# A hybrid attention and state-space layer: the context's norm and the state space's parameters made among the first norms

## The chip, the core and the metric

The kernel runs on one core of a Trainium2 chip. The metric is device time in microseconds for one execution. A core has five engines with instruction queues of their own: TensorE (PE, its weight loads are shown as PEld), VectorE (DVE), ScalarE (ACT), GpSimd (POOL) and SyncE (SP), which issues most of the transfers here. Everything is fp32; where a product must be exact enough, each factor is split into a high and a low part and three matmuls are made of one.

## What is computed

One layer of a diffusion backbone over 1024 tokens and 256 context tokens of 1024 channels. The part of the reference that matters:

```python
mod_x = silu(c) @ w_mod + b_mod;  mod_c = silu(c_ctx) @ w_mod + b_mod
px = modulate(rmsnorm(x, g_norm_mix), sh1, sc1) @ w_in
pc = modulate(rmsnorm(ctx, g_norm_mix), ch1, cc1) @ w_in
y_conv = conformer_conv(conv_x, ...);  y_fnet = fourier_mix(fnet_x, ...)
y_na   = neighbourhood_attention(q, k, v, kc, vc, rpb)
y_ssm  = s5_bidirectional(ssm_x, ssm_c, a_re, a_im, log_dt, b, c, d, ...)
out = group_rmsnorm(concat(y_conv, y_fnet, y_na, y_ssm)) @ w_out + b_out
x = x + gt1 * out;  x = x + gt2 * mlp(modulate(rmsnorm(x), sh2, sc2))
```

The state space (S5) has 16 groups of 16 channels with 64 complex states in two directions. Its context scan runs first and gives the token scan its first state. From a_re, a_im and log_dt come, once for the layer, the step's decay and angle, their powers up to 9, and the discretised B: here called the parameters.

## The kernel before, in words

`body` traces the whole program. A planner then sets the order of the instructions on each engine: it keeps to the data's dependencies and the tiles' buffers, prefers what was traced earlier, and lets later work in where an engine would stand idle by its own estimates. Waits between engines are put in by the framework. Only from the attention on is TensorE's order written out by hand, and in the MLP that of four engines. So a step that stands earlier in the source has precedence there, and does not have to run there. Each engine's queue is in order once it is made; `tc.issue_after(ins)` makes what its block traces on the engine of `ins` stand behind `ins`.

The stages, by what they compute:

- First norms (from L297). x is loaded in two halves of 512 tokens, its squares are summed (ACT and DVE, L206 to L210). For each of eight channel chunks k the shift and scale are made on TensorE from `wmodA` (`gemv`, L149 and L155; loads L299; `set_mod` L160, `gsc` L316), and the chunk is normalised in `normchunk`: `nt` on DVE (L215), `xh` on ACT (L218), `xl` on DVE (L220). The weights of tiles 12, 13 (state space) and 8 (keys) are loaded in this loop and split by ACT (L233) and POOL (L235).
- Tokens' projections: `x_tile` makes 24 matmuls (L364) for a tile of 128 output channels and one half. First come tiles 12, 13 and 8 for both halves; `ev_ssm` writes the state-space channels to `us_d` in DRAM, `ev_k` the keys to `k_d`.
- Context: `ctt` (L401) is loaded into a pool opened after the first norms' pool is closed; then four modulation blocks, the context's norm (`modnorm`), and its projections `c_tile` (L242 to L244) for tiles 12 and 13 (stored to `us_d` by L423) and 8 (`k_ctx`), then five modulation blocks. A modulation block (`mods`, L340 to L357) loads 512 KB of `wmodB` into a buffer that the weights share (three buffers), makes a gemv on TensorE (L344), copies the row on ACT and turns it with two small matmuls (L349).
- Parameters (L436 to L581): some ninety small operations on POOL (`E_ = G`) and DVE, 16 columns wide, hopping between the two; two sines on ACT; powers `pw` by `cmul`, copied to `pa` and `pb` by DVE (L552 to L556); `bb` and `bm` on POOL.
- State space, eight batches of two groups: `ssm_setup` (L607 to L651: tables of weights on POOL and DVE, kernel matmul `pk` L635, transposes `pt`, copies on ACT, and a trip of the kernel through DRAM), `ssm_tables` (phases and sines, L656 to L672), `ssm_main` (`U` from `us_d` L679, state matmul `ps` L686, a rotation and scan on DVE and POOL L692 to L709, output matmul `py` L713 to L717, store to `ys_d`).
- Filling in beside it and behind it: one modulation block, tile 9 (keys), tiles 4 and 5 (Fourier) with two blocks behind each half, the values (L760), the first convolution input `conv_in(0)` (its gate is L787), the state space's output gate (GLU), the Fourier mixing, `conv_in(1)`, the queries (tiles 6 and 7) with a modulation block behind each half, and the convolution's taps of the first half of the channels (L1012 to L1023, one DVE instruction of 512 columns a tap).
- Attention with the output projection beside it (its first DVE step is L1249), then the MLP.

`mods` makes 16 blocks at most in this phase; the other 16 are made in the attention.

## Time and profile before

| what | value |
|---|---|
| median of 3 runs | 1310.3 us (1308.32 to 1315.78) |
| the profiled execution | 1304.56 us, span 1302.6 us |
| TensorE busy in the span | 1184.6 us (91%) |
| DVE, POOL, ACT busy | 1003.8, 767.1, 645.0 us |
| mean granted TensorE clock | 0.954 of full speed (2.4 GHz) |

The profile is of one execution. Times in it count from the start of the span. A line number L is that of the kernel's file; a helper that makes many instructions gives them all one line, so names of tiles matter as much. "Busy" says nothing of why an engine is idle; the views of waits name the instruction whose end was waited for. The granted clock is the share of full speed that TensorE was allowed; it has two levels, 1.2 and 2.4 GHz, and a mean between them says how long it was at which.

### The profile page before, as it was taken

Reading aid. Unit: us, or ns where it says so; the run is one execution under the profiler, and the core shown is the slowest. Engines: PE = TensorE matmul, PEld = TensorE weight load, DVE = VectorE, ACT = ScalarE, POOL = GpSimd, SP = SyncE. Lnnn points to the kernel's source line nnn. Section 1 sums busy time; section 2 is a strip of 40 time slices with the busy share of each in tenths; the row PEclk is TensorE's granted clock in tenths of the full one; section 3 lists DMA queues with packets and bytes.
Section 4 is the critical chain, followed back from the end, with each engine's and each line's share of the span. In section 5 each row is a group of like instructions: output and inputs, shape, how many; then the busy total and the mean of one; then the engine's idle time right before and its main releaser. Section 6 shows DMA issues by size and latency. Waiting matters only on the chain.

```text
span 1302.6 us, 18800 instructions
## 1 busy us (share of the span) xinstructions
PE 1184.6 (91%) x6252; PEld 962.1 (74%) x6252; DVE 1003.8 (77%) x1604; ACT 645.0 (50%) x1335; POOL 767.1 (59%) x1004
## 2 busy tenths in 40 slices
PE   4988988998866898998999999999999999999995
PEld 2776677876646787877777788888887888877875
DVE  5557789689988868758696487787787787787767
ACT  5343343323345655644664355555445555445564
POOL 2138787472556733015268377777777777777654
PEclk9888989998975999998999999999999999999998
DMA  9455342261154644324021111112211111211113
GB/s 362 139 193 157 101 121 70 68 204 55 41 165 136 172 134 119 114 81 146 25 74 41 57 51 38 52 56 65 65 53 37 50 57 65 65 40 42 57 41 130
DMA packets 75058, 121.75 MB, mean 93 GB/s; under 512 B 16977, under 2 KB 35154, under 8 KB 74962
## 3 DMA queue, kind: packets, MB, share of 16 engines
q1 hardware_dynamic: 62802, 113.22, 27.9%
q10 hardware_dynamic: 12160, 7.34, 1.8%
q8 instruction: 49, 0.80, 0.3%
q14 instruction: 47, 0.39, 0.1%
HBM read 106.66 MB, written 13.88 MB: 93 GB/s over the span
## 4 chain that ended last, share of the span: by engine, by line
PE 57%; DVE 21%; ACT 6%; DMA 4%; issue 3%; POOL 3%; SPq 0%; ACTq 0%; DVEq 0%; POOLq 0%
PE fa L1477 12%; PE qa L1477 6%; PE fb L1477 6%; PE qb L1477 6%; DVE cacc L1020 3%; PE qc L1477 3%; PE fc L1477 3%; PE p_t L1275 2%; PE mm L1102 2%; PE mm L1477 2%; PE f L1477 1%; DMA kr<-k_d 1%; PE p_t L1263 1%; DVE fl L1493 1%; PE mm L364 1%
## 5 line engine op out<-in xcount | busy, mean ns | idle before, releaser
L1461 POOL TENSOR_TENSOR w2l<-w2r,w2h 128x128 fp32r<-128x128 f32 (+1 forms) x232 | 174.1, 752 | 78.0 <-ACT w2h L1460 71.8
L1498 DVE SCALAR_TENSOR_TENSOR X<-fa,gt2c,X 128x512 f32<-128x512 f32 x216 | 159.5, 745 | 14.4 <-PE fa L1477 14.4
L1460 ACT ACTIVATE w2h<-w2r 128x128 fp32r<-128x128 f32 (+1 forms) x232 | 85.9, 387 | 134.3 <-POOL w2r L1714 69.7
L235 POOL TENSOR_TENSOR wlo<-wraw,whi 128x1024 fp32r<-128x1024 f32 x30 | 73.6, 2456 | 120.0 <-ACT whi L233 96.5
L1461 POOL TENSOR_TENSOR w2l<-w1r,w2h 128x256 fp32r<-128x256 f32 x136 | 102.2, 766 | 65.2 <-ACT w2h L1460 41.3
L1498 DVE SCALAR_TENSOR_TENSOR X<-fb,gt2c,X 128x512 f32<-128x512 f32 x108 | 80.6, 746 | 41.5 <-PE fb L1477 40.7
L1461 POOL TENSOR_TENSOR w2l<-ws,w2h 128x256 fp32r<-128x256 f32 x84 | 68.0, 816 | 39.1 <-ACT w2h L1460 20.4
L1020 DVE SCALAR_TENSOR_TENSOR cacc<-cv,wdw,cacc 128x512 f32<-128x512 f32 x92 | 87.2, 994 | 0.4
L364 PE MATMUL mm<-xh,whi 128*128 128x512 f32 x192 | 79.0, 428 | 6.4 <-ACT xh L218 4.8
L364 PE MATMUL mm<-xl,whi 128*128 128x512 f32 x192 | 80.5, 419 | 0.5 <-DVE xl L220 0.5
L364 PE MATMUL mm<-xh,wlo 128*128 128x512 f32 x192 | 79.6, 416 | 0.0
L1460 ACT ACTIVATE w2h<-w1r 128x256 fp32r<-128x256 f32 x136 | 54.0, 410 | 51.0 <-DVE w1r L1614 19.7
L1477 PE MATMUL qa<-cb,w2h 128*128 128x512 f32 x224 | 70.6, 396 | 0.7 <-ACT ft L1629 0.7
L1477 PE MATMUL fa<-th,w2h 128*128 128x512 f32 x156 | 62.1, 398 | 0.0
L1477 PE MATMUL fa<-th,w2l 128*128 128x512 f32 x156 | 61.4, 393 | 0.7 <-POOL w2l L1461 0.7
L1477 PE MATMUL fa<-tl,w2h 128*128 128x512 f32 x156 | 61.5, 394 | 0.0
L1018 POOL TENSOR_TENSOR pacc<-pacc,ptmp 128x512 f32<-128x512 f32 x24 | 39.6, 1649 | 27.7 <-ACT ptmp L1017 27.7
L1460 ACT ACTIVATE w2h<-ws 128x256 fp32r<-128x256 f32 x84 | 33.1, 410 | 42.7 <-DVE ws L1610 19.6
L364 PEld LDWEIGHTS mm<-xh,whi 128*128 128x128 f32 x192 | 38.2, 201 | 17.5 <-ACT xh L218 5.3
L1477 PEld LDWEIGHTS qa<-cb,w2h 128*128 128x128 f32 x224 | 42.0, 188 | 11.3 <-ACT ft L1629 1.1
L233 ACT ACTIVATE whi<-wraw 128x1024 fp32r<-128x1024 f32 x30 | 31.7, 1056 | 31.9 <-DMA wraw<-in_w_out 10.6
L1498 DVE SCALAR_TENSOR_TENSOR X<-fc,gt2c,X 128x512 f32<-128x512 f32 x56 | 41.9, 749 | 6.9 <-PE fc L1477 2.4
(799 smaller groups left out, 3847.0 us busy)
## 6 DMA issues: line engine op xcount, KB each, us to landing
w2r<-in_w_ff SPq DMA_DIRECT2D x68, 256.0 KB
wmB<-in_wmodB SPq DMA_DIRECT2D x32, 512.0 KB
w1r<-in_w_ff SPq DMA_DIRECT2D x64, 256.0 KB
wm<-in_wmodA SPq DMA_DIRECT2D x16, 512.0 KB
wraw<-in_w_in SPq DMA_DIRECT2D x12, 512.0 KB
x<-in_xT SPq DMA_DIRECT2D x8, 512.0 KB
wraw<-in_w_out SPq DMA_DIRECT2D x8, 512.0 KB
kr<-k_d SPq DMA_DIRECT2D x16, 256.0 KB
```

Source lines behind the costliest of these rows:

```text
L233: S.activation(hi, raw, AF.Copy)
L235: (lo_eng or G).tensor_tensor(lo, raw, hi.bitcast(F32), ALU.subtract)
L364: PE.matmul(o, a_[:, k, :], b_[hf][k], start=k == 0 and i == 0, stop=k == 7 and i == 2)
L1018: G.tensor_tensor(pacc, pacc, t, ALU.add)
L1020: V.scalar_tensor_tensor(acc, x(k), w(k), acc, ALU.mult, ALU.add)
L1102: PE.matmul(o, a_[:, 2 * kk + c, :], b_, start=c == 0 and i == 0, stop=c == 1 and i == 2)
L1263: PE.transpose(pT[:, i * P:(i + 1) * P], pr_[:, i * P:(i + 1) * P], ident)
L1275: PE.matmul(po[:, j * 64:j * 64 + 64], ptt[:, i * P:(i + 1) * P], rv, start=i == 0, stop=i == 4, skip_group_check=True)
L1460: S.activation(hi, a, AF.Copy)
L1461: G.tensor_tensor(lo, a, hi.bitcast(F32), ALU.subtract)
L1477: PE.matmul(o, a_[:, i, :], m_, start=start and j == 0, stop=stop and j == 2, skip_group_check=True)
L1498: return V.scalar_tensor_tensor(x, o, gt2(k), x, ALU.mult, ALU.add).ins
```

## The change

- A pool `xc` for the context is opened ahead of the first norms' pool. `ctt` is loaded into it in front of the modulation weights of chunk 3 (k == 3), the context's squares and reciprocal root are made at k == 5, and its eight chunks are normalised right behind the loop. `ctt`, `ch` and `cl` keep their shapes.
- The state space's parameters become a function, traced behind the norm of chunk 1. Their five loads (`log_dt` twice, B twice, C) stand behind the identity's and ahead of the first modulation weights. The arithmetic is the same; the eight copies into `pa` and `pb` go from DVE to POOL. `ssm_setup` becomes a function traced earlier (it is called where it was), and its tiles `ca`, `cx`, `kt_`, `tz`, `wt` move to the pool opened after the parameters' small pool is closed.
- Behind the first norms the order is: tiles 12 and 13 for both halves, the context's tiles 12 and 13, tile 8 for both halves, the context's tile 8. The nine modulation blocks that stood there are taken out.
- Of the 16 modulation blocks nine are now traced with tiles 9, 4 and 5, one behind `conv_in(0)`, one ahead of `conv_in(1)`, four with the queries, the rest ahead of the taps. SP's part of the block with tiles 9, 4 and 5 (their loads but for tile 9's weights, which stand ahead) is queued behind the first load of `U`.

The diff, without the lines that only move:

```diff
+    cts = ExitStack()
+    xc = open_pool("ctxc", "left", stack=cts)
...
+    def ssm_loads():
+        ldt = tn("ldt")
+        for d in range(2):
+            SP.dma_start(ldt[d * 64:(d + 1) * 64, :], ap(A["log_dt"], d * 16, [[0, 64], [1, 16]]))
...
+        for i in range(2):
+            SP.dma_start(bn[i], A["bnat"][:, i, :])
+        SP.dma_start(cn, A["cnat"])
...
+    def ssm_params():
...
         for dst, src in ((pa_r, pw_r), (pa_i, pw_i)):
-            V.tensor_copy(dst[0:64], src[0:64])
-            V.tensor_copy(dst[64:128], src[64:128, ::-1, :])
+            G.tensor_copy(dst[0:64], src[0:64])
+            G.tensor_copy(dst[64:128], src[64:128, ::-1, :])
...
     load_x(0)
     SP.dma_start(ident, A["cst"][:, 0:P])
+    ssm_loads()
+    ctt = []
     for k in range(8):
+        if k == 3:
+            for i in range(8):
+                ctt.append(xc.tile([P, TC], F32, name="ctt", tag="hc", bufs=16))
+                SP.dma_start(ctt[i], A["ctxT"][:, i, :])
         wm = load_wm(k)
...
         norm_x(0, pbs[0], k)
+        if k == 1:
+            ssm_params()
...
+        if k == 5:
+            pbc = rstd_bc(xc, sumsq(xc, ctt, TC), TC, 0, st_tile, NM)
+            pbs.append(xc.tile([P, TC], F32, name="pbc"))
+            S.copy(pbs[2], pbc[:, :TC])
+    ch, cl = zip(*[normchunk(xc, ctt[k], TC, gsc[:, k, 1:2], mod[:, 0, k, 1:2], pbs[2], "c", "hc", xc) for k in range(8)])
     st.close()
...
-    for hf in range(2):
-        for ti in FIRST:
-            o = x_tile(cw[ti], hf, (("mm", "gn"), ("at", "gv"))[hf][ti == 8])
...
-    mods(4)
-    ch, cl = modnorm(xp, sumsq(xp, ctt, TC), ctt, TC, ...
+    for hf in range(2):
+        for ti in FIRST[:2]:
+            ev_ssm(ti - 12, hf, x_tile(cw[ti], hf, first_tag(ti, hf)))
     for m in range(2):
         o = c_tile(cw[12 + m])
...
+    for hf in range(2):
+        ev_k(8, hf, x_tile(cw[8], hf, first_tag(8, hf)))
+    gvp = ps_tile("gv", "gvp")
...
     k_ctx(8)
-    mods(5)
...
-            SP.dma_start(U[:, g, 0:160], ap(us_d, ...
+            ld = SP.dma_start(U[:, g, 0:160], ap(us_d, ...
+        state_in.append(ld.ins)
...
-    mods(1)
     cw[9] = load_w(A["w_in"][9])
-    for hf in range(2):
-        ev_k(9, hf, x_tile(cw[9], hf))
-    k_ctx(9)
-    mods(0)
-    for ti in (4, 5):
-        w = load_w(A["w_in"][ti])
+    with tc.issue_after(state_in[0]):
+        mods(1)
         for hf in range(2):
-            ev_u(ti, hf, x_tile(w, hf))
-            mods(2)
+            ev_k(9, hf, x_tile(cw[9], hf))
+        k_ctx(9)
+        for ti in (4, 5):
+            w = load_w(A["w_in"][ti])
+            for hf in range(2):
+                ev_u(ti, hf, x_tile(w, hf))
+                mods(2)
...
     conv_in(0)
+    mods(1)
...
+    mods(1)
     conv_in(1)
...
-    mods(1)
+    mods(2)
     for _ in tap_steps(0, 0):
```

## Rows read from the trace of the kernel before

**Rows 1.** The page's first part: busy time, share of the span, instructions
```profile
PE 1184.6 (91%) x6252; PEld 962.1 (74%) x6252; DVE 1003.8 (77%) x1604; ACT 645.0 (50%) x1335; POOL 767.1 (59%) x1004
```

**Rows 2.** Windows by stage: PE, PEld, DVE, ACT, POOL busy; granted clock; DMA share, GB/s
```profile
37.00:78.00 41.00, 40.74 (x226) 30.72 (x225) 21.07 (x45) 12.66 (x24) 2.57 (x7) 0.94 0.42 132
78.00:130.00 52.00, 42.95 (x360) 34.07 (x362) 36.39 (x94) 22.50 (x55) 37.93 (x90) 0.80 0.59 187
130.00:205.00 75.00, 64.54 (x475) 49.75 (x472) 62.49 (x90) 30.63 (x68) 60.82 (x67) 0.95 0.36 108
205.00:264.50 59.50, 59.20 (x405) 50.59 (x404) 42.64 (x76) 20.12 (x42) 32.12 (x37) 0.97 0.25 72
264.50:391.00 126.50, 99.84 (x444) 80.81 (x443) 120.12 (x148) 46.17 (x70) 65.23 (x38) 0.89 0.36 115
```

**Rows 3.** Timeline of DVE: start, us, engine, line, operation, out<-in, count, [idle before it <-releaser]
```profile
264.59 0.69 DVE L787 SCALAR_TENSOR_TENSOR cv<-cth,mm 128x512 f32<-128x512 f32 x1 [5.75 <-PE mm L364]
...
391.10 0.82 DVE L1249 CUSTOM_DVE_ANT_0 pr__3575<-p_s,bt 128x640 f32<-128x640 f32 x1
```

**Rows 4.** Chain of waits, 98 to 131 us: start, duration, what
```profile
99.52 4.52 DMA us_d<-pC
...
104.47 3.15 DMA us_d<-pC
```

**Rows 5.** Timeline of SP, POOL and DVE: the parameters
```profile
69.32 1.20 SPq L446 DMA_DIRECT2D t_ldt<-in_log_dt  x2
...
73.56 0.20 POOL L451 TENSOR_SCALAR t_dn<-t_ldt 128x16 f32<-128x16 f32 x1 [34.68 <-DMA t_ldt<-in_log_dt]
...
102.75 0.71 DVE L553 COPY pa_i<-pw_i 64x160 f32<-64x160 f32 x1
```

**Rows 6.** Views by tile: state matmul, output matmul; first and last start
```profile
L686 PE MATMUL ps<-U,wt x128: 297/298/350, 129.7 to 243.8; 128*64 128x159 f32 x128
...
L717 PE MATMUL py<-hr,cx x64: 273/275/421, 143.5 to 258.4; 128*128 128x128 f32 x64
```

**Rows 7.** Windows, the parameters' new and old place
```profile
18.00:37.00 19.00, 12.87 (x75) 7.61 (x76) 14.13 (x23) 9.72 (x17) 4.38 (x2) 0.86 0.90 347
73.50:106.00 32.50, 26.79 (x259) 21.50 (x257) 20.40 (x72) 14.96 (x38) 20.86 (x72) 0.84 0.59 184
```

**Rows 8.** Waits of PE, 70 to 265 us: in total, times, longest
```profile
PE pg L344 <- DMA wmB<-in_wmodB: 3.5, 1, 3.5
...
PE ps L686 <- ACT wt L651: 2.5, 1, 2.5
...
PE pg L344 <- ACT gv_rows L357: 1.4, 1, 1.4
```

**Rows 9.** Timeline of PE behind a gap; chain of waits at 248
```profile
116.02 0.63 PE L364 MATMUL mm<-xh,whi 128*128 128x512 f32 x1
...
116.86 0.40 PE L364 MATMUL mm<-xh,wlo 128*128 128x512 f32 x1
...
247.99 8.64 PE mm L364 x37
```

**Rows 10.** Timeline of PE: one modulation block
```profile
99.26 0.39 PE L349 MATMUL gvp<-cst,gv_rows 128*128 128x2 f32 x2
99.58 0.64 PE L344 MATMUL gvp<-wmB,sT 128*32 128x128 f32 x16
```

**Rows 11.** Timeline of SP, 15 to 60 us
```profile
15.56 1.67 SPq L570 DMA_DIRECT2D bn<-in_bnat  x2
...
27.12 23.68 SPq L299 DMA_DIRECT2D wm<-in_wmodA  x8
```

**Rows 12.** Timeline: a DVE instruction beside a POOL split and alone
```profile
110.04 2.19 DVE L660 TENSOR_SCALAR p<-ph 128x318 f32<-128x318 f32 x1 [0.20 <-ACT ph L659]
...
120.18 0.32 DVE L660 TENSOR_SCALAR p<-ph 128x318 f32<-128x318 f32 x1
...
109.61 2.43 POOL L235 TENSOR_TENSOR wlo<-wraw,whi 128x1024 fp32r<-128x1024 f32 x1
```

More of the change, by code (lines that the diff above doesn't have):

```diff
@@ L306, in add_rstd, with tn @@
         S.copy(pbs[hf], rstd_bc(p1, pbs[hf], H, 0, (mm_tile, at_tile)[hf], NS))
+    sset = ExitStack()
+    sp = open_pool("ssm", "right", stack=sset)
+    tst = ExitStack()
+    tp = open_pool("tiny", "right", stack=tst)
+    GB = 2
+    NB_ = 16 // GB
+    fl = lambda t: t.rearrange("p g q -> p (g q)")
+    v4 = lambda t: t.rearrange("p g (s m) -> p g s m", m=16)
+    b3 = lambda t: t.rearrange("p (g m) -> p g m", g=16)
+    PR = {}
+    def tn(name, pool=None):
+        return (pool or tp).tile([P, 16], F32, name="t_" + name)
@@ new lines, in ssm_loads @@
+    def ssm_loads():
+        ldt = tn("ldt")
+        for d in range(2):
+            SP.dma_start(ldt[d * 64:(d + 1) * 64, :], ap(A["log_dt"], d * 16, [[0, 64], [1, 16]]))
+        bn = [sp.tile([P, 2, 160], F32, name="bn", tag="ss", bufs=4).rearrange("p a b -> p (a b)")[:, :256]
+              for _ in range(2)]
+        cn = sp.tile([P, 2, 256], F32, name="cn")
+        for i in range(2):
+            SP.dma_start(bn[i], A["bnat"][:, i, :])
+        SP.dma_start(cn, A["cnat"])
+        PR["loads"] = ldt, bn, cn
@@ L397, in body @@
     SP.dma_start(colf, A["cols"][:, NCOLS - 40:])
-    ctt = []
-    for k in range(8):
-        ctt.append(xp.tile([P, TC], F32, name="ctt", tag="hc", bufs=16))
-        SP.dma_start(ctt[k], A["ctxT"][:, k, :])
-    for hf in range(2):
-        for ti in FIRST:
-            o = x_tile(cw[ti], hf, (("mm", "gn"), ("at", "gv"))[hf][ti == 8])
-            if ti >= 12:
-                ev_ssm(ti - 12, hf, o)
-            else:
-                ev_k(ti, hf, o)
-    gvp = ps_tile("gv", "gvp")
-    mods(4)
-    ch, cl = modnorm(xp, sumsq(xp, ctt, TC), ctt, TC,
-                     lambda k: gsc[:, k, 1:2], lambda k: mod[:, 0, k, 1:2], "c", "hc", xp, pt=st_tile)
     def c_tile(w):
@@ L561, in body @@
-    tt(rho, rho, rho, ALU.mult)
-    E_.tensor_scalar(th8, tau, 8.0, 1.0, ALU.mult, ALU.mult)
-    frac(th8)
-    E_.tensor_scalar(th_h, th8, 1536.0, 1536.0, ALU.add, ALU.subtract)
-    tt(th_l, th8, th_h, ALU.subtract)
-    bn = [sp.tile([P, 2, 160], F32, name="bn", tag="ss", bufs=4).rearrange("p a b -> p (a b)")[:, :256]
-          for _ in range(2)]
-    cn = sp.tile([P, 2, 256], F32, name="cn")
-    for i in range(2):
-        SP.dma_start(bn[i], A["bnat"][:, i, :])
-    SP.dma_start(cn, A["cnat"])
@@ L572, in body @@
-    b3 = lambda t: t.rearrange("p (g m) -> p g m", g=16)
-    bc16 = lambda t: t[:, :, None].to_broadcast([P, 16, 16])
-    bb_r = sp.tile([P, 16, 16], F32, name="bb_r")
-    bb_i = sp.tile([P, 16, 16], F32, name="bb_i")
-    cmul(bb_r, bb_i, bc16(zr), bc16(zi), b3(bn[0]), b3(bn[1]), None, "ss", G)
-    tst.close()
-    bm = sp.tile([P, 2, 16, 32], F32, name="bm")
-    G.memset(bm[:, :, :, 16:32], 0.0)
-    G.tensor_copy(bm[:, 0, :, 0:16], bb_r)
-    G.tensor_copy(bm[:, 1, :, 0:16], bb_i)
-    GB = 2
@@ L721, in ssm_main @@
             S.dma_start(ap(ys_d, (GB * b + g) * 16 * 1024, [[128, 8], [1024, 16], [1, 128]]), yt[:, g, :])
+    rho, th_h, th_l = PR["rho"], PR["th_h"], PR["th_l"]
+    for _ in range(3):
+        new_cx(sp2)
     ready = [ssm_setup(0) + ssm_tables(0)]
```

347 lines of the change are left out of this document (178 added, 169 removed).

## The prediction

> **What bounds the kernel now.** I read the page first, then the stages, then the waits of the second and third stage. By the page TensorE is busy for 91% of the span [rows 1]. That is an average, and the change touches only what lies before the attention, so I cut the span into stages [rows 2]. The reader is to see three kinds. From 37 to 78 us TensorE is full (40.74 of 41.00 us) and POOL nearly empty (2.57). From 78 to 130 TensorE has holes (42.95 of 52.00), its granted clock falls to 0.80, and POOL is busy with small things. From 264.5 to 391 DVE is full (120.12 of 126.50) and TensorE isn't. After 391 come attention and MLP, which the change leaves alone. So the question is when DVE's last stage can begin: it begins with the convolution's gate at 264.59 us, after an idle 5.75 us that ended with the TensorE tile of that gate [rows 3]. Whatever brings that tile forward brings the end forward.
>
> What holds it back is in the chain of waits [rows 4]: at 99.52 and 104.47 us it stands on the two stores of the context's projected channels into us_d (4.52 and 3.15 us), then on DVE's and ACT's setup work. The parameters are late because log_dt is asked for at 69.32 us only; POOL sits idle for 34.68 us before its first use, and the last power copy is done at 102.75 + 0.71 = 103.46 [rows 5]. The first state matmul (ps) starts at 129.7, the last output matmul (py) at 258.4 [rows 6].
>
> **Parameters and context norm, moved.** In the old place, from 73.5 to 106, POOL is busy 20.86 us and DVE 20.40 us, DVE's with the context's norm [rows 7]; eight power copies go from DVE to POOL, about 0.5 us each by the last one's 0.71. In the new place they stand beside 37 to 78, where DVE is idle for 41.00 - 21.07 = 19.9 us and POOL for 38 [rows 2]: they fit, at no cost of their own. What the move frees on TensorE is the gaps of 78 to 130, which sum to 52.00 - 42.95 = 9.05 us. The waits say why [rows 8]: the longest are modulation matmuls waiting for their weights (3.5) or for a copy (1.4), because nothing else is ready while the context's tiles wait for their norm. In the new order the projections of the tokens (tiles 8 and 9) stand there. I take 8 us; between 4 (half the waits come back) and 9.
>
> **Clock.** Granted 0.80 over those 52 us means 1.2 GHz for 2 x 0.20 = 40% of them; 40% of 42.95 busy us is 17.2, of which half, 8.6, is what the low clock cost. The level was low behind a 3.5 us wait [rows 8] and came back when TensorE had been busy again (the same matmul takes 0.63 us, then 0.40) [rows 9]. With the gaps gone I take 7; between 3 and 8.6.
>
> **Modulations.** Before, the 16 modulation blocks of this phase are issued ahead of the first convolution input. After it, nine are issued among tiles 9, 4 and 5 and seven behind the first convolution input, in the stage where TensorE has 126.50 - 99.84 = 26.7 idle us. A block is 0.64 us of gemv and 0.39 us of selection [rows 10], overlapping slightly: 7 x 0.95 = 6.6 us leave the path to 264.5 (5 to 7). Their seven weight loads and copies move with them and fall under DVE's taps; if that cover fails, because they share a PSUM bank with the group norms, it costs the 6.6 again.
>
> **The state space's lead.** Setup of batch 0 no longer waits for the context, so wt is there before U. The 2.5 us that ps once waited for wt [rows 8], and about 1.5 us of low clock behind that gap, go: 4 us. The bounds are 0 and everything that 130 to 264.5 still holds: 10.5 + 0.3 idle, and 3.8 + 1.8 from clocks 0.95 and 0.97 [rows 2], 16 us in all. I take the small value because the other waits there are of the batches on themselves (hr, Ss, yt).
>
> **The added wait.** The modulations' loads and the weights of tiles 4 and 5 are queued on SP behind batch 0's U load, which waits for the pC stores. TensorE waits for them. The cover is tiles 8 and 9 with their context parts: 24 matmuls at 8.64/37 = 0.234 us [rows 9] are 5.6 us a tile, four tiles and two half-width context tiles 28 us. No cost.
>
> **The start.** The price of the change is here. On SP five small loads go ahead of the first modulation weights, for which TensorE waits first of all: at (1.20 + 1.67)/4 = 0.72 us an issue [rows 5, 11] 3.6 us. Eight context loads (8 x 128 KB, so 3.0 us at the 347 GB/s of 18 to 37 us [rows 7]) go ahead of the fourth, but SP spends 23.68 us there issuing eight loads into buffers that aren't free [rows 11]. On DVE 18 to 37 us is 14.13 of 19.00 busy [rows 7] and the parameters are issued ahead of the third norm chunk: some 26 links of 16 columns, at a quarter of the 160-column copy (0.71 us [rows 5]), are 4.6 us. Nothing hides what falls before 37, for TensorE is full behind it. I take 3 us; at best 0, at worst 4.6 + 3.6 + 3.0 = 11.2.
>
> Contention enters here too: with POOL's split running, DVE's phase rounding took 2.19 us where the same one took 0.32 without it [rows 12]. The Trainium skill (GPSIMD Engine Reference, Key points) says that POOL shares its SBUF interfaces with VectorE and contends with instructions of two SBUF inputs; that speaks against putting the parameters beside the norms. By these rows the trace agrees, for large POOL operations. If DVE's chunk steps were held for as long as POOL works on the parameters (20.86 us [rows 7]), the sum below would be 22.6 - 20.9 = 1.7 us; that is the third case's time and is counted there. The links are 16 columns wide, so I keep the 3.
>
> **The sum.** 8 + 7 + 6.6 + 4 - 3 = 22.6 us; the ends are 4 + 3 + 5 + 0 - 11.2 = 0.8 and 9 + 8.6 + 7 + 16 - 0 = 40.6. Against the profiled execution, 1304.6 us (span 1302.6), that is 1282.0. That execution lies 5.7 us under the median of the runs, 1310.3, so the median comes to 1287.7, say 1288.
>
> **Rivals.** *The whole lead.* TensorE's full stretch ends at 78 [rows 2]; with a pC store (3.15 to 4.52 us [rows 4]) and U's load behind it the first ps could start at about 85 instead of 129.7. If TensorE's order was held up by the state space all the way, the remaining holes of 130 to 264.5 close too: 40.6 us, 1270. For it: before 130 the chain of waits is on stores and setup, not on TensorE [rows 4]. Against: from 205 on TensorE is full (59.20 of 59.50), so the lead of 45 us can't be used beyond the holes. 0.14.
>
> *Given back (the third case).* The order of instructions on each engine is made by a planner with its own costs. If it puts the same work a little differently into 264.5 to 391, where DVE has only 6.4 us of slack, the 20 us turn into later taps or into norms that wait for modulations. Also here: norms held by POOL's links; and the change moves the trace of the program, but the planner could leave the parameters where they run now, since they are only as early as DVE and POOL find room. Time 1304 to 1310, no change. 0.22, a little over half of it (0.12) within 0.5%.
>
> *Slower.* One mechanism: the parameters as a chain in front of the norms. They hop between POOL and DVE some thirty times, and took from 73.56 to 103.46, 30 us with their waits [rows 5]. Each engine runs its queue in order, so a link that waits for the other engine holds the norm chunks behind it, and TensorE behind those. If all of it stood ahead of chunk 2, TensorE would fill 30 us later; against the 25.6 us of gain this is 4 us slower, and with the seven modulations uncovered 11: 1321. It decides from 25.6 us of delay on; DVE's 19.9 idle us between 37 and 78 [rows 2] say that the chunks have slack of their own, so I think a tenth of it, the 3 us of the sum, likelier. 0.12.
>
> **How the numbers follow.** Forecast 0.52, whole lead 0.14, given back 0.22, slower 0.12. A change under 0.5% (6.5 us) can't be told from none, since the three runs alone span 7.5. Faster: 0.52 + 0.14 + 0.10 of the third case = 0.76. Same: 0.12 of the third and 0.02 of the fourth, 0.14. Slower: the fourth's other 0.10. The forecast's own range is 1275 to 1301; to leave out no more than 2 in 10 the range goes from 1269 (1310.3 - 40.6) to 1309 (1310.3 - 0.8, which takes in most of the given-back case).
>
> **What the next profile would show.** Right: log_dt's loads before 10 us and POOL's small operations before 60; pC stored by 85; first ps before 95; no TensorE gap over 2 us from 78 to 114 and a granted clock above 0.9 there; the convolution's gate at about 242 and its stage as long as now; the first DVE step of attention (now 391.10 [rows 3]) at about 368. Wrong: TensorE's full stretch beginning after 42 instead of 37 (the start costs more); gate at 242 but attention at 390 (given back at DVE); first ps early but the gate unmoved (TensorE, not the state space, was the bound and the clock stays low).

## The result, and the profile after

The change makes the kernel slower: 1319.1 us (median of 7 runs, 1315.24 to 1324.52) against 1310.3 before (7 runs), a ratio of 1.0081 with a 95% interval of 1.0052 to 1.011. The prediction of 1288 (1269 to 1309) was wrong in sign. The profiled execution has a span of 1317.2 us, 14.6 more than before; of that, 5.7 us are the distance of the profiled execution of before from its median.

TensorE has hardly more to do, by the first part of the page of the kernel after (before: [rows 1]):

```profile
PE 1191.2 (90%) x6252; PEld 965.9 (73%) x6252; DVE 989.7 (75%) x1596; ACT 650.7 (49%) x1340; POOL 776.2 (59%) x1012
```

So the stages must tell. The kernel after in windows (columns as in [rows 2]; the last two begin at the gate and at attention's first step):

```profile
0.00:37.00 37.00, 17.00 (x93) 11.18 (x93) 22.98 (x65) 22.29 (x40) 24.05 (x72) 0.79 0.94 336
37.00:78.00 41.00, 35.84 (x203) 26.42 (x203) 26.29 (x53) 11.76 (x21) 19.83 (x26) 0.86 0.32 106
78.00:130.00 52.00, 46.35 (x287) 35.58 (x283) 38.90 (x66) 27.02 (x54) 32.54 (x37) 0.93 0.39 114
130.00:205.00 75.00, 63.57 (x478) 48.19 (x476) 65.84 (x103) 28.32 (x69) 56.12 (x64) 0.91 0.33 101
205.00:272.20 67.20, 62.44 (x420) 53.84 (x421) 27.65 (x51) 20.91 (x37) 32.42 (x31) 0.95 0.44 142
272.20:394.50 122.30, 101.97 (x541) 81.50 (x540) 112.16 (x150) 46.57 (x74) 44.88 (x27) 0.88 0.39 123
394.50:645.30 250.80, 214.49 (x1401) 184.45 (x1400) 178.95 (x335) 135.29 (x247) 101.60 (x71) 0.91 0.38 116
```

The first two stages of the kernel before, the second of which stands in [rows 2]:

```profile
0.00:37.00 37.00, 19.41 (x111) 12.45 (x112) 20.14 (x39) 20.33 (x33) 10.28 (x11) 0.93 0.91 340
```

In the first 37 us POOL's work has grown from 10.28 to 24.05 us, and TensorE's has shrunk from 19.41 to 17.00. From 37 to 78 TensorE, full before (40.74 of 41.00), is busy 35.84. From 78 to 130 its work is denser (46.35 against 42.95) at a clock of 0.93 instead of 0.80: there the change does what was forecast, in part. The gate comes at 272.2 instead of 264.6, attention at 394.5 instead of 391.1. The kernel after in DVE's timeline, at both places:

```profile
268.04 2.31 DVE L248 TENSOR_TENSOR yl<-ysb,yh 128x1024 fp32r<-128x1024 f32 x1 [17.50 <-ACT yh L247]
270.63 1.69 DVE L248 TENSOR_TENSOR yl<-ysb,yh 128x1024 fp32r<-128x1024 f32 x1 [0.28 <-ACT yh L247]
272.24 0.67 DVE L813 SCALAR_TENSOR_TENSOR cv<-cth,mm 128x512 f32<-128x512 f32 x1
...
393.26 0.17 DVE L594 SCALAR_TENSOR_TENSOR mod<-gvp,cols 128x16 f32<-128x16 f32 x1 [7.55 <-PE gvp L592]
394.54 0.82 DVE L1277 CUSTOM_DVE_ANT_0 pr__3581<-p_s,bt 128x640 f32<-128x640 f32 x1 [1.10 <-PE p_s L1275]
```

Two new things stand on DVE. Ahead of the gate it makes the low part of the GLU's input (`yl`), and waits 17.50 us for it; before, the gate waited for TensorE's tile alone [rows 3]. And ahead of attention's first step stands the last modulation's selection, for which DVE waits 7.55 us; before there was no such wait [rows 3]. TensorE's tile for the gate ends at 269.7 here (269.27 + 0.39, its 72nd matmul of the convolution's input), against 264.5 before.

**One account.** To compare TensorE's stages I add up, up to the gate, its idle time and an estimate of what the low clock cost (busy time times one minus the granted clock), from the means of two profiles of each kernel:

| stage | before: idle, clock | after: idle, clock | difference |
|---|---|---|---|
| 0 to 78 us | 17.8, 1.9 | 26.2, 8.1 | +14.6 |
| 78 to 130 | 8.0, 9.5 | 5.6, 3.2 | -8.7 |
| 130 to the gate | 11.3, 3.8 | 16.8, 8.9 | +10.6 |

That is 16.5 us more loss, less seven modulation blocks (6.6 predicted) that now run behind the gate: 9.9. The gate moved from a mean of 263.6 to 273.45, by 9.85; of this TensorE's tile moved 6.9 (its end from a mean of 263.5 to 270.4) and 3 are the GLU's split in front of the gate. The account is rough: the clock's term alone differs by 3.8 us up to 78 between the two profiles of the kernel before, and over all kernels below, the gate's time less the loss lies between 203 and 215, for the planner puts different work ahead of the gate. Only differences of several us mean something.

Behind the gate, by means of the same profiles: up to attention 5.3 us shorter, from there to the MLP 8.9 longer, the rest 2.0 shorter.

### The profile page after: what moved, and what is told of

The parts are those of the page before. It is cut to its first block, busy times and chain, and to the rows that moved or that the text cites. A ratio compares the mean times of both kernels' runs of the same rounds, so it can differ in the third digit from the quotient of the medians.

```text
span 1317.2 us, 18804 instructions
## 1 busy us (share of the span) xinstructions
PE 1191.2 (90%) x6252; PEld 965.9 (73%) x6252; DVE 989.7 (75%) x1596; ACT 650.7 (49%) x1340; POOL 776.2 (59%) x1012
## 4 chain that ended last, share of the span: by engine, by line
PE 60%; DVE 20%; DMA 8%; ACT 5%; issue 3%; POOL 3%; SPq 1%; ACTq 0%; DVEq 0%; POOLq 0%
PE fa L1505 12%; PE qa L1505 6%; PE fb L1505 6%; PE qb L1505 6%; DVE cacc L1048 5%; PE mm L607 4%; PE mm L1505 3%; PE qc L1505 3%; PE fc L1505 3%; DMA wraw<-in_w_out 2%; PE p_t L1303 2%; PE f L1505 2%; PE mm L1130 2%; PE p_t L1291 1%; DVE Ss L724 1%
## 5 line engine op out<-in xcount | busy, mean ns | idle before, releaser
L1489 POOL TENSOR_TENSOR w2l<-w2r,w2h 128x128 fp32r<-128x128 f32 (+1 forms) x232 | 171.2, 740 | 72.0 <-ACT w2h L1488 67.4
L1526 DVE SCALAR_TENSOR_TENSOR X<-fa,gt2c,X 128x512 f32<-128x512 f32 x216 | 159.7, 746 | 13.7 <-PE fa L1505 13.7
L1048 DVE SCALAR_TENSOR_TENSOR cacc<-cv,wdw,cacc 128x512 f32<-128x512 f32 x92 | 81.9, 930 | 0.8
L1046 POOL TENSOR_TENSOR pacc<-pacc,ptmp 128x512 f32<-128x512 f32 x24 | 36.6, 1524 | 27.3 <-ACT ptmp L1045 27.3
L1505 PEld LDWEIGHTS qa<-cb,w2h 128*128 128x128 f32 x224 | 42.0, 188 | 11.3 <-ACT ft L1657 1.1
L607 PEld LDWEIGHTS mm<-xh,wlo 128*128 128x128 f32 x192 | 37.7, 197 | 15.8 <-POOL wlo L235 6.3
```

The source lines that it names most:

```text
L607: PE.matmul(o, a_[:, k, :], b_[hf][k], start=k == 0 and i == 0, stop=k == 7 and i == 2)
L1046: G.tensor_tensor(pacc, pacc, t, ALU.add)
L1048: V.scalar_tensor_tensor(acc, x(k), w(k), acc, ALU.mult, ALU.add)
L1489: G.tensor_tensor(lo, a, hi.bitcast(F32), ALU.subtract)
L1505: PE.matmul(o, a_[:, i, :], m_, start=start and j == 0, stop=stop and j == 2, skip_group_check=True)
L1526: return V.scalar_tensor_tensor(x, o, gt2(k), x, ALU.mult, ALU.add).ins
```

## The experiments

The main theory: the early parameters delay the weight splits on POOL and with them TensorE's start, so that TensorE and not the state space sets the gate. Rivals: the context's loads on SP; the moved modulations; the hold behind the first load of `U`. A row of the table is one kernel; "gate" and "attention" are the two steps above, "MLP" its first matmul, in us of its profile.

| kernel | gate | attention | MLP | median (runs) | ratio to before (95%) |
|---|---|---|---|---|---|
| before | 264.6 | 391.1 | 630.4 | 1310.3 (7) | |
| before_again | 262.6 | 391.5 | 634.3 | 1310.9 (1) | |
| after | 272.2 | 394.5 | 645.3 | 1319.1 (7) | 1.0081 (1.0052 to 1.011) |
| after_again | 274.7 | 397.1 | 646.1 | 1319.0 (1) | |
| params_late | 268.7 | 392.5 | 639.3 | 1316.8 (12) | 1.005 (1.003 to 1.007) |
| params_split | 266.8 | 379.3 | 626.3 | 1300.4 (8) | 0.9924 (0.9895 to 0.9954) |
| split_loads | 267.2 | 382.9 | 631.5 | 1302.6 (11) | 0.9935 (0.9914 to 0.9956) |
| ctx_hold | 269.7 | 393.3 | 640.8 | 1312.5 (12) | 1.0034 (1.0011 to 1.0056) |
| ctx_hold_split | 258.3 | 384.0 | 626.3 | 1300.4 (10) | 0.9941 (0.9916 to 0.9967) |
| no_hold | 275.5 | 399.3 | 641.1 | 1322.1 (6) | 1.0096 (1.0058 to 1.0133) |
| mods_back | 287.7 | 397.7 | 643.4 | 1317.6 (9) | 1.0075 (1.005 to 1.0099) |
| both_back | 282.3 | 392.8 | 639.4 | 1313.6 (12) | 1.0032 (1.0007 to 1.0056) |
| both_split | 276.8 | 389.4 | 635.0 | 1307.0 (12) | 0.9978 (0.9948 to 1.0009) |
| mods_alone | 253.5 | 407.3 | 655.8 | 1329.9 (5) | 1.0155 (1.0126 to 1.0183) |
| mods_mid | 271.8 | 391.2 | 645.3 | 1316.8 (7) | 1.0054 (1.0034 to 1.0075) |
| mid_split | 266.5 | 383.9 | 631.7 | 1306.2 (12) | 0.9973 (0.9951 to 0.9996) |
| after_bank | 276.0 | 392.0 | 634.3 | 1310.1 (12) | 1.0019 (0.9995 to 1.0043) |
| hold_split_bank | 265.0 | 382.6 | 631.7 | 1305.0 (12) | 0.9977 (0.9955 to 0.9999) |
| hold_split_mid | 265.7 | 380.6 | 626.5 | 1301.8 (12) | 0.9945 (0.9926 to 0.9965) |
| split_gate | 256.8 | 386.9 | 633.7 | 1306.8 (12) | 0.9964 (0.9945 to 0.9982) |

The ratio is to runs of the kernel before that were taken beside each kernel; their medians lie between 1308.7 and 1311.2, so medians of two rows that differ by two or three us are not told apart.

**How far a profile can be trusted.** The two kernels again, unchanged.

> The kernel before once more, unchanged, for a second profile. The first profiled execution lay 5.7 us under its median. Theory: the difference sits in attention, where the output weights that are loaded beside the window's values landed 5.5 to 6.3 us after they were asked for (8 to 9 in the changed kernel); a second profile shows 1306 to 1312 with attention's first step to the first fused matmul at 242 to 247 us instead of 239.3, and all up to 391 us within 1 us of the first. Rival: the same times all along as in the first profile, 239.3 there, and then the changed kernel's 250.8 is all its own.

> The changed kernel once more, for a second profile. All up to attention's first step (394.5 us) within 1.5 us of the first; attention's first step to the first fused matmul 246 to 252 us (250.8), since the landing of the output weights scatters by some us from one execution to the next, and the rest 672 to 675.

Gates repeat within 2.5 us (264.6 and 262.6; 272.2 and 274.7), where 1 and 1.5 had been expected, so the shift of about 10 us is real. The quick part of the first profile of before is its attention, 239.3 us against 242.8.

**The parameters on POOL.** First they go back behind the context's norm, then they stay early in the trace but queue behind the third weight split on POOL.

The edit of params_late:

```diff
-    ssm_loads()
...
-        if k == 1:
-            ssm_params()
...
+    ssm_loads()
+    ssm_params()
     st.close()
```

> The changed kernel with the parameters' loads and arithmetic behind the loop of the first norms again; context norm, tile order and modulations as changed. POOL theory: the parameters stand on POOL ahead of the second and third weight split (42.43 and 52.24 us, before the change 28.75 and 34.98), TensorE stands idle or at a low clock for it from 20 to 52 us. Without them the second and third split lie before 40 us, TensorE is full from about 40, and the gate comes 5 to 9 us earlier than 272.2, although the state space starts later: span 1308 to 1312. Rival (the eight early context loads and the context's norm in the loop cost the start): splits and TensorE's start stay within 3 us of the changed kernel, gate 269 or later, span 1314 or more. Second rival (the early parameters pay by the state space's lead): gate later than 272.2, span above 1318.

The edit of params_split:

```diff
-        (lo_eng or G).tensor_tensor(lo, raw, hi.bitcast(F32), ALU.subtract)
+        cur["split"] = (lo_eng or G).tensor_tensor(lo, raw, hi.bitcast(F32), ALU.subtract).ins
...
-        if k == 1:
-            ssm_params()
+        if k == 3:
+            with tc.issue_after(cur["split"]):
+                ssm_params()
```

> The changed kernel with the parameters still early, but only behind the third weight split on POOL. POOL theory: the three splits lie before 40 us, TensorE is full from about 40 as with the parameters late, and the state space keeps most of its lead (first state matmul before 118 us): gate 264 to 268, span 1308 to 1313. Rival (loads ahead of the first modulation weights and the context's loads set the start): gate within 2 us of 272.2, span 1315 to 1319.

POOL's timeline of the kernel before has its second and third split here:

```profile
28.75 2.36 POOL L235 TENSOR_TENSOR wlo<-wraw,whi 128x1024 fp32r<-128x1024 f32 x1 [11.06 <-ACT whi L233]
34.98 2.35 POOL L235 TENSOR_TENSOR wlo<-wraw,whi 128x1024 fp32r<-128x1024 f32 x1 [3.87 <-ACT whi L233]
```

All three of the kernel after, with the first parameter:

```profile
10.46 0.21 POOL L347 TENSOR_SCALAR t_dn<-t_ldt 128x16 f32<-128x16 f32 x1 [6.87 <-DMA t_ldt<-in_log_dt]
...
19.88 2.35 POOL L235 TENSOR_TENSOR wlo<-wraw,whi 128x1024 fp32r<-128x1024 f32 x1
...
42.43 2.82 POOL L235 TENSOR_TENSOR wlo<-wraw,whi 128x1024 fp32r<-128x1024 f32 x1
...
52.24 2.37 POOL L235 TENSOR_TENSOR wlo<-wraw,whi 128x1024 fp32r<-128x1024 f32 x1
```

And the second and third of params_split:

```profile
30.81 2.35 POOL L235 TENSOR_TENSOR wlo<-wraw,whi 128x1024 fp32r<-128x1024 f32 x1 [10.82 <-ACT whi L233]
37.65 2.36 POOL L235 TENSOR_TENSOR wlo<-wraw,whi 128x1024 fp32r<-128x1024 f32 x1 [4.49 <-ACT whi L233]
40.09 0.20 POOL L347 TENSOR_SCALAR t_dn<-t_ldt 128x16 f32<-128x16 f32 x1
```

Before and in params_split each split waits for ACT, its input: POOL is idle ahead of it. After, the splits carry no wait in brackets: POOL comes to them straight from the parameters, the second 13.7 us later than before. Its input `whi` was made by ACT at 34.13 us, so POOL's queue held it for 8.3 us; the rest is the later load and copy of these weights. TensorE stands for it in its timeline of the kernel after:

```profile
45.31 0.79 PE L607 MATMUL mm<-xh,wlo 128*128 128x512 f32 x1 [4.22 <-POOL wlo L235]
```

The matmul behind that gap takes 0.79 us, where one takes 0.40 at the clock's higher level [rows 9]. TensorE's waits from 0 to 78 us (in total, times, longest), first of the kernel before, then of the kernel after:

```profile
PE pg L149 <- DMA wm<-in_wmodA: 11.0, 1, 11.0
```

```profile
PE pa L183 <- DVE acc L210: 14.0, 2, 12.8
PE mm L607 <- ACT xh L218: 5.6, 2, 5.3
PE mm L607 <- POOL wlo L235: 4.2, 1, 4.2
```

The wait for `wlo` (4.2 us, 5.5 in after_again) is the largest part of the 8.4 us by which TensorE's idle time up to 78 has grown; before and in params_split there is none.

With the same arithmetic queued behind the splits the median falls by 18.7 us, to 1300.4, faster than both kernels: that the parameters' place decides the sign is shown. That POOL alone does it is not: with the work on POOL the parameters' links on DVE move too, and no run separates the two. The first norm chunk on DVE, before and after (20.13 in params_split):

```profile
18.34 0.75 DVE L215 SCALAR_TENSOR_TENSOR nt<-x,gsc,acc 128x512 f32<-128x512 f32 x1
```

```profile
22.36 0.77 DVE L215 SCALAR_TENSOR_TENSOR nt<-x,gsc,acc 128x512 f32<-128x512 f32 x1
```

Where the 18.7 come from is less clear, for the planner re-orders what follows: TensorE's tile for the gate ends at 259.0, 11.4 us earlier than after's mean, and there is no wait for a modulation ahead of attention, which begins 16.5 us earlier. By the account the loss falls by only 3.6 us up to 78, and by 7.9 from 130 to the gate. So the start is at most a part of it, and params_late says the same: there the loss up to 78 falls by 8.1 us (second and third split at 33.53 and 41.63), more than in params_split, but the median by 2.3 only, to 1316.8 (a span of 1314.8, where 1308 to 1312 had been expected); its attention still waits 9.6 us for a modulation.

**The loads on SP.** Five parameter loads behind the first modulation weights, the context's at k == 5; then instead the context's loads alone behind the weights'.

split_loads, on top of params_split:

```diff
-    ssm_loads()
     ctt = []
...
         if k == 0:
             SP.dma_start(cst, A["cst"][:, P:])
+            ssm_loads()
...
-        if k == 3:
+        if k == 5:
             for i in range(8):
```

> Parameters behind the third weight split, and their five loads behind the first modulation weights, the context's loads two steps later. Start theory: the first modulation weights are asked for at 3.9 us (8.20 in the changed kernel), TensorE's first matmul comes at 11 us instead of 12.8 to 14.6, the gate 2 to 4 us earlier than 266.8: span 1295 to 1298. Rival (the queue's order does not matter, since the first norms wait for DVE and POOL): gate within 1 us of 266.8, span 1298 to 1301.

ctx_hold (with params_split as well it is ctx_hold_split):

```diff
-        SP.dma_start(raw, src)
+        cur["load"] = SP.dma_start(raw, src).ins
...
-                SP.dma_start(ctt[i], A["ctxT"][:, i, :])
+                with tc.issue_after(cur["load"]):
+                    SP.dma_start(ctt[i], A["ctxT"][:, i, :])
```

> The changed kernel with the context's eight loads behind the third projection weight on the sync engine's queue (in the changed kernel they stand from 16.78 to 26.9 us, ahead of the second). Loads theory: the second weight is asked for at about 21 us instead of 26.11, idle time and low clock of TensorE up to 78 us (33.8 us in the changed kernel, 20 in the one before) shrink by 2 to 5 us, the gate comes at 268 to 270, span 1312 to 1316. Rival (POOL's order alone decides: the second weight's split waits for the parameters until 42.4 whenever its load lands): gate 272 to 275, span 1316 to 1319.

> The parameters behind the third weight split, and the context's loads behind the third weight load. Loads theory: the three splits at 17, 26 and 32 us (17.6, 30.8 and 37.7 with the parameters behind the splits alone), TensorE's loss up to 78 us 26 us or less (30.7), gate 262 to 265, span 1293 to 1297. Rival (the context's norm then comes late and holds the context's projections, as in the kernel before): first gain lost again before 130 us, gate 266 to 270, span 1298 to 1304.

SP's timeline of the kernel after shows what these loads stand in front of:

```profile
16.78 8.29 SPq L547 DMA_DIRECT2D ctt<-in_ctxT  x7
26.11 0.33 SPq L231 DMA_DIRECT2D wraw<-in_w_in  x1
```

In ctx_hold the second weights are asked for at 20.76, the second split starts at 39.96 instead of 42.43, the loss up to 78 falls from 34.3 to 26.4 (1.2 of it idle time, the rest the clock's estimate) and the median by 6.6 us. Together with params_split the gate comes at 258.3, 8.5 earlier than in params_split, but the median stays at 1300.4, as with params_split alone: its attention waits 6.58 us for a modulation again. split_loads gained nothing over params_split.

**The hold behind U.**

```diff
-    with tc.issue_after(state_in[0]):
+    if True:
```

> The changed kernel without the hold: tiles 9, 4 and 5 with their nine modulation blocks may be issued ahead of the first state load U. Prediction's step (the hold costs nothing, tiles 8 and 9 cover it): gate 271 to 273, span 1315 to 1319. Rival (TensorE's waits for the state space from 130 us on, 8.2 us for hr and 6.7 us for U, stand there because the hold has pushed tiles 9, 4 and 5 back; or the reverse, without it the tiles' loads and stores delay U): gate more than 3 us off 272.2 to either side.

1322.1 us: not faster without it, so the added wait costs nothing, as predicted.

**The modulations.** Back ahead of the first convolution input; the move alone, on the kernel before; and the combinations.

mods_back (with params_late both_back, with params_split both_split):

```diff
                 ev_u(ti, hf, x_tile(w, hf))
-                mods(2)
+                mods(4)
...
     conv_in(0)
-    mods(1)
...
-            mods(1)
...
-    mods(2)
     for _ in tap_steps(0, 0):
```

> The changed kernel with all its modulation blocks among tiles 9, 4 and 5, ahead of the first convolution input; nothing else undone. Ring theory: the seven blocks behind the convolution hold the three buffers that the output weights also need, so the first two output weights are asked for at 384.65 and 397.13 us (before the change: 261.45 and 340.84), and gate to end of attention takes 373.1 us where it took 365.8. With the blocks back ahead, the two loads are asked for before 350 us, the convolution's gate moves from 272.2 to about 279 (7 blocks x 0.95 us) and gate to end of attention returns to about 366: the two cancel, profile span 1313 to 1319, same as the changed kernel. Rival (the planner's new order lengthens attention whatever the blocks do): gate at 279 and the 373 stay, span about 1324.

> The changed kernel with both undone: the parameters behind the loop of the first norms and all modulation blocks ahead of the convolution. What is left of the change is the context's early load and norm, the tile order and the hold. If moving the modulations moves time from one stage to another and no more (1317.6 against 1319.1 us in the changed kernel), this is the kernel with late parameters (1316.8) within 3 us: gate 280 to 286, gate to attention 108 to 114, span 1311 to 1317. Rival (the two parts hinder each other, and the rest of the change pays by itself): span under 1309.

> The parameters behind the third weight split and all modulation blocks ahead of the convolution. By the same reading the gate is at 280 to 284, gate to attention 106 to 112, and the span that of the kernel with the parameters behind the splits (1298.8) within 4 us. Rival (seven blocks less ahead of the gate are worth their 6.6 us there and nothing is given back once the parameters are out of the way): span 1303 to 1308.

With the parameters behind the splits the move of the modulations pays: with the blocks back ahead of the gate (both_split) the median is 1307.0, 6.6 us above params_split, where DVE waits for none of them ahead of attention. Elsewhere it doesn't: both_back, 1313.6, is 3.2 below params_late, and mods_back is no slower than after. In both_back what is left of the change is the context's early norm, the tiles' order and the hold; by its ratio, 1.0032 (1.0007 to 1.0056), these do not pay by themselves. No kernel here takes the context's norm alone out of the first norms, so what it costs there stays open.

mods_alone, on the kernel before:

```diff
-    mods(4)
...
-    mods(5)
...
     conv_in(0)
+    mods(1)
...
+    mods(1)
     conv_in(1)
...
-    mods(1)
+    mods(2)
     for _ in tap_steps(0, 0):
```

> The kernel before with only the modulation blocks moved, as the change has them: nine around tiles 9, 4 and 5, seven behind the first convolution input. Prediction's step: gate 6.6 us earlier (258) and the end with it, span 1296. Ring theory: gate at 258, but the first output weights asked for after 370 us and gate to end of attention 373 instead of 366, so that the gain is given back: span 1300 to 1305.

The move alone brings the gate forward by 10 us and attention back by 16: +20 us in all, the worst kernel of the study. Its windows and DVE's timeline (gate to attention; then the wait):

```profile
253.50:407.30 153.80, 121.57 (x579) 93.61 (x578) 126.78 (x165) 48.59 (x78) 72.53 (x44) 0.81 0.37 118
```

```profile
405.99 0.17 DVE L351 SCALAR_TENSOR_TENSOR mod<-gvp,cols 128x16 f32<-128x16 f32 x1 [12.22 <-PE gvp L349]
```

Against [rows 2] TensorE is busy 21.7 us longer in that stage, at a clock of 0.81 instead of 0.89, and DVE ends it waiting 12.22 us. In mods_back the trade goes the other way: the gate 14.2 us later than after's mean, attention 110.0 us behind it instead of 122.35, and the same median within the intervals. The chain of waits of the kernel after tells why the blocks come so late (start, us, what):

```profile
378.22 1.33 DVE yf L259 x2
...
379.69 1.11 PE pg L587 x16
...
380.82 3.83 DMA wmB<-in_wmodB
384.65 8.94 DMA wraw<-in_w_out
```

The gemv into `pg` at 379.69 waited for `yf`, a step of the group norm on DVE, which works in the same PSUM bank; only when it had run could its weight buffer take the next block, and the first output weights, which share these buffers, are asked for at 384.65 (261.45 before). To test the bank, the gemvs leave it; and the later blocks are moved right behind `conv_in(0)`, under the taps.

after_bank (with ctx_hold and params_split hold_split_bank):

```diff
-pg = gvp[:, 0:P] if i % 2 else ps_tile("gn", "pg", P)
+pg = gvp[:, 0:P] if i % 2 else gvp[:, P:2 * P]
```

mods_mid (with params_split mid_split, with ctx_hold too hold_split_mid), the three later calls of `mods` taken out:

```diff
     conv_in(0)
-    mods(1)
+    mods(8)
...
```

> The changed kernel with one address changed: the even modulation blocks accumulate in free columns of the bank that the odd ones use, and no longer in the group norms' bank. Bank theory: the blocks need not wait for the second yf norm (378 us), their weights are asked for before it, DVE's wait of 7.5 us for the last block goes, the first output weights are asked for before 370 us; attention begins at 382 to 388 us (394.5 and 397.1 in the two profiles), span 1304 to 1311. Rival (the weights' ring and the sync queue hold the blocks back, whatever the bank): attention at 392 or later, span 1315 to 1319.

> The changed kernel with its seven late modulation blocks all directly behind the first convolution input, ahead of the group norms, instead of spread up to the taps. Bank theory: in the changed kernel the last blocks wait for the group norms' PSUM bank (9.50 us on a norm at 378 us), then their weights are asked for one by one, and DVE waits 7.5 us for the last one ahead of attention's first step. Placed ahead of the group norms nothing of this is left: DVE's wait for the last block is gone, attention begins at 383 to 389 us (394.5), the first output weights are asked for before 360 us, span 1302 to 1310. Rival (the seven blocks only take TensorE's place from the convolution's other inputs): attention at 393 or later, span 1315 or more.

> Both repairs: parameters behind the third weight split, and the seven blocks directly behind the first convolution input. If the two causes are separate and add, the gate is at 267 as with the parameters behind the splits (1298.8 us of span), attention begins at 374 to 379 and the state of the output weights is as early as in the kernel before: span 1292 to 1298. Rival (the last blocks' wait was already gone with the parameters behind the splits, which had no DVE wait for a modulation): no further gain, span 1298 to 1303.

> Context's loads held, parameters behind the splits, and the modulation blocks off the group norms' bank. That kernel without the last edit has its gate at 258.3 us and attention at 384.0, with DVE waiting 6.6 us for the last block. Bank theory: gate 258, attention 372 to 378, span 1285 to 1292. Rival (DVE is full in this stage and its order fills the wait's place with other work): attention 381 to 384, span 1293 to 1298.

> The same, but with the seven blocks directly behind the first convolution input instead of off the bank. Gate 258, no wait of DVE for the last block, gate to attention 117 as with the blocks there before: attention 374 to 377, span 1287 to 1294. Rival (the blocks take TensorE and the ring from the next inputs, as much as the wait cost): attention 380 to 384, span 1293 to 1299.

after_bank in DVE's timeline:

```profile
390.39 0.17 DVE L594 SCALAR_TENSOR_TENSOR mod<-gvp,cols 128x16 f32<-128x16 f32 x1
390.51 1.54 DVE L1048 SCALAR_TENSOR_TENSOR cacc<-cv,wdw,cacc 128x512 f32<-128x512 f32 x2
391.97 0.82 DVE L1277 CUSTOM_DVE_ANT_0 pr__3573<-p_s,bt 128x640 f32<-128x640 f32 x1
```

The wait is gone, taps fill its place, and the kernel takes 1310.1 us, 9.0 less than after, though its gate is no earlier (276.0). So the edit is worth 9 us in the change as it stands; that the wait for the bank is worth them is not shown. Attention begins at 392.0, 3.8 us earlier than after's mean, where the bank theory had 382 to 388; the larger part comes behind it, 242.3 us from attention to the MLP instead of 249.9. And mods_mid, in which DVE waits for no modulation either and the first output weights are asked for at 303.71, takes 1316.8, only 2.3 less than after.

The Trainium skill (Perfetto Trace Analysis, Optimizing Tensor Performance, Matmuls) advises that independent matmul groups rotate through different PSUM banks. after_bank, faster by 9.0 us, agrees; hold_split_bank does not: ctx_hold_split has a wait of 6.58 us for a modulation, the other bank takes it away, and the median is 1305.0 instead of 1300.4, with the gate at 265.0 instead of 258.3. hold_split_mid (1301.8) misses its expected gain too, and mid_split (1306.2) is slower than params_split. The 9 us of the bank's edit and params_split's 18.7 are not to be added up.

**The gate on DVE.** In params_split TensorE has the gate's tile ready at 259.0, and the gate runs at 266.8. Its DVE timeline says why:

```profile
258.68 1.22 DVE L248 TENSOR_TENSOR yl<-ysb,yh 128x1024 fp32r<-128x1024 f32 x1 [18.13 <-ACT yh L247]
265.17 1.71 DVE L248 TENSOR_TENSOR yl<-ysb,yh 128x1024 fp32r<-128x1024 f32 x1 [5.26 <-ACT yh L247]
266.80 0.67 DVE L814 SCALAR_TENSOR_TENSOR cv<-cth,mm 128x512 f32<-128x512 f32 x1
```

So the GLU's split goes behind the first gate in DVE's queue, on top of params_split:

```diff
+            cur.setdefault("gate", gate)
...
-        split(yh, yl, ysb, V)
+        with tc.issue_after(cur["gate"]):
+            split(yh, yl, ysb, V)
```

(`gate` is the gate's instruction.)

> params_split with the low part of the GLU's input (yl, on DVE) queued behind the first convolution gate. In params_split the gate at 266.8 stands on DVE behind the second yl at 265.17, which waited for ACT and for the load of ysb (DVE idle 18.13 and 5.26 us), while TensorE had finished the gate's tile at about 259. Theory that the queue of DVE, not TensorE, sets the gate there: gate at about 259 to 260, some 7 us earlier, attention earlier by 3 to 7 (372 to 376), median 1293 to 1297. Rival, that something else sets attention's 379 (total work of DVE, or the load of ysb itself): gate early all the same, attention at 378 to 382, median 1299 to 1303. Rival, that TensorE sets the gate: gate unmoved at 265 to 267.

Its DVE timeline:

```profile
256.80 0.69 DVE L814 SCALAR_TENSOR_TENSOR cv<-cth,mm 128x512 f32<-128x512 f32 x1 [18.56 <-PE mm L608]
257.40 1.22 DVE L248 TENSOR_TENSOR yl<-ysb,yh 128x1024 fp32r<-128x1024 f32 x1
268.96 1.23 DVE L248 TENSOR_TENSOR yl<-ysb,yh 128x1024 fp32r<-128x1024 f32 x1 [8.31 <-ACT yh L247]
```

The gate comes 10 us earlier and waits for TensorE again: the queue did hold it. But attention comes 7.6 us later (386.9), with 6.1 us of waiting for a modulation, and the median is 1306.8. The theory that the gate's stall is worth its length at the end fell: the stall moved to the second `yl` (8.31 us) and to the modulation.

## Why the prediction was wrong

The forecast put the gate at 242; it came at 273.5, the mean of two profiles. The steps, by the account above:

- **The start** (predicted -3, bounds 0 to 11.2; measured -14.6, outside them). This step failed. It and its rival priced the parameters as links on DVE, in front of the norm chunks. That came in part (the first chunk is 4.0 us late), but what neither had is POOL: there the parameters stood in front of the weight splits, which [rows 7] gave as 4.38 busy us and the prediction passed over; an almost idle engine was read as a free one. "POOL for 38" idle us between 37 and 78 did not help, because the work was put before 37. The context's loads, costed at 3.0 by bytes, held the next weights on SP; ctx_hold gives back 7.9 us of loss, params_split 3.6, both together 8.5. What makes the other 6.1 is open; the context's squares and norm, which every variant of the change keeps there, are untested. "SP spends 23.68 us there" anyway was no cover: what is late is what stands behind in the queue.
- **Gaps and clock, 78 to 130** (8 + 7; measured 2.4 + 6.3). The clock's term was right, the gaps' was mis-sized: TensorE still stands idle 5.6 us there.
- **The state space's lead** (4, bounds 0 to 16; measured -10.6). The parameters were early, but the two pC were stored at 100.46 and 105.77, not by 85, and no earlier than before [rows 4]. The 85 took for granted that the first norms' stretch still ended at 78; it now ends 15 us later. The modulation rows' copies, by tile, of the kernel before:

```profile
L152 ACT COPY gv_rows<-pg x8: 353/372/375, 15.2 to 63.9; 128x256 f32<-128x256 f32 x8
```

and of the kernel after, with its state and output matmuls [rows 6]:

```profile
L152 ACT COPY gv_rows<-pg x8: 352/372/374, 16.6 to 79.1; 128x256 f32<-128x256 f32 x8
...
L709 PE MATMUL ps<-U,wt x128: 298/298/499, 112.9 to 231.0; 128*64 128x159 f32 x128
...
L740 PE MATMUL py<-hr,cx x64: 273/275/421, 134.9 to 241.0; 128*128 128x128 f32 x64
```

The last copy is 15.2 us late, which fits: 85 + 15 is the 100 at which the first pC was stored. The state space still starts 16.8 us earlier and ends 17.4 earlier, while the gate is later: this is the clause "TensorE, not the state space, was the bound", but for the 3 us of the GLU's split. TensorE meets new waits there, in the kernel after from 130 us to the gate (in total, times, longest):

```profile
PE py L739 <- DVE hr L731: 8.2, 4, 4.7
PE ps L709 <- DMA U<-us_d: 6.7, 2, 3.6
```

With the parameters behind the splits the loss there is 17.8 instead of 25.7, and the wait for `U` 0.5 instead of 6.7. Why params_late keeps 24.3 stays open.
- **The modulations** (6.6; before the gate they came, behind it they cost more). "If that cover fails, because they share a PSUM bank with the group norms, it costs the 6.6 again": it failed: the wait is there, in the bank that the clause names, and the move costs 20 us when made alone. With the parameters out of the way the cover held, and the move gains the 6.6 (both_split to params_split). The clause priced their work, not the wait behind the norms and the weights that are then loaded one by one; what that wait is worth is not isolated (9.0 us by after_bank, 2.3 by mods_mid).
- **The added wait** (no cost): right, by no_hold.
- **From the gate on** ("whatever brings that tile forward brings the end forward"): not so. In the seven kernels with the parameters behind the splits and the modulations not moved back, the gate lies at 257 to 267 and attention at 379 to 387; the three earliest gates of the study (mods_alone, split_gate, ctx_hold_split) all end in a wait for a modulation, of 12.2, 6.1 and 6.6 us. What sets 379 is open. From attention to the MLP it takes 239 to 254 us over all kernels. Of the 8.9 us that the change adds there, 4.4 are TensorE's waits for the copies `ptt` on ACT (13.3 and 14.3 us in the two profiles before, 19.8 and 16.6 after; 11.2 in after_bank, 19.2 in mods_mid); why these come late is open too.

The third case ("given back") and the slower one each held part of the truth: part of the loss came from in-order queues, as in the latter, and the modulations' wait from the former. The slower case had 0.12, too little, because its decision rested on DVE's slack alone. That its 1321 lies near the measured 1319.1 is luck: it has the norm chunks held for 30 us, and the first was held for 4.0.

## What to carry to other kernels

Work of a few us on an almost idle engine is not free if that engine's queue is in order and something short that feeds the bound stands behind it: look for the next instruction in that queue and for who waits for it, and queue the new work behind that one (18.7 us here, of which the start accounts for 3.6). Moving work out of a full stretch can gain its length or lose more than that in a new wait for a PSUM bank or a weight buffer where it goes: moving these blocks was worth 6.6 us in one kernel and cost 20 in another. An earlier milestone is worth what the next wait lets through.

## What the hardware showed that was not expected

A 16-column POOL operation that takes 0.21 us alone takes over three times as long when DVE adds 512-column tiles, in POOL's timeline of the kernel after:

```profile
25.44 0.74 POOL L362 TENSOR_TENSOR t_rho<-t_rho 128x16 f32<-128x16 f32 x1
...
27.13 0.21 POOL L362 TENSOR_TENSOR t_rho<-t_rho 128x16 f32<-128x16 f32 x1
```

Both rows have the same form. At 25.44 DVE begins two additions of 1.48 us together, shown below; at 27.13 DVE is idle, from 26.91 to 27.42. In the other direction, a 2-column DVE operation lasted as long as a whole split of POOL; DVE's timeline of the kernel after:

```profile
19.95 2.30 DVE L553 TENSOR_SCALAR gsc<-mod,cols 128x2 f32<-128x2 f32 x1
...
25.43 1.48 DVE L210 TENSOR_TENSOR acc<-acc,sq 128x512 f32<-128x512 f32 x2
...
56.12 0.23 DVE L553 TENSOR_SCALAR gsc<-mod,cols 128x2 f32<-128x2 f32 x1
```

The split ran from 19.88 to 22.23, the small step from 19.95 to 22.25; the same step takes 0.23 at 56.12. So a small step on either engine can wait out a large one on the other, and the prediction's price of a link, a quarter of a 160-column copy, left that out. The Trainium skill (GPSIMD Engine Reference, Key points) says that GpSimd shares its SBUF interfaces with VectorE and contends with VectorE instructions that have two SBUF inputs; the additions are such, and the trace agrees. The small DVE step has one tensor input, as has the phase rounding of [rows 12], which the prediction took for this condition: for two inputs it is the additions that show it, and not those rows.
